# Turning the feed-forward's gated activations with VectorE blocks and a trip through DRAM, in place of TensorE transposes

## The chip, the cores and the metric

The kernel runs on one core of a Trainium2 chip, in one launch. The metric is the device time of that launch in microseconds (us), as the median of several runs. Beside it stands one profiled execution, whose span (first to last instruction) and own time are given; every view of the trace shown here comes from that execution.

## The reference

The reference is a trunk of two layers over 256 tokens of width 1024 in float32. A layer is a half-step feed-forward, a token mixer (gated DeltaNet beside a causal Conformer convolution), and a second half-step feed-forward, each between an RMS norm ahead and one behind. Cut to what the change concerns:

```python
def swiglu_ffn(h, w_in, w_out):
    gate, up = jnp.split(h @ w_in, 2, axis=-1)      # h: 256 x 1024, w_in: 1024 x 5632
    return (jax.nn.silu(gate) * up) @ w_out         # w_out: 2816 x 1024

for i in range(DEPTH):                              # DEPTH = 2
    f = swiglu_ffn(rmsnorm(x, ffn1_norm_pre[i]), ffn1_w_in[i], ffn1_w_out[i])
    x = x + 0.5 * rmsnorm(f, ffn1_norm_post[i])
    ...                                             # the token mixer
    f = swiglu_ffn(rmsnorm(x, ffn2_norm_pre[i]), ffn2_w_in[i], ffn2_w_out[i])
    x = x + 0.5 * rmsnorm(f, ffn2_norm_post[i])
```

There are thus four feed-forwards. The product `silu(gate) * up` comes out with tokens on the partitions, and the second matrix product needs it as the stationary operand, with its 2816 channels on the partitions: it has to be transposed.

## The kernel before

**Products.** Every float32 product is made of three TensorE products of rounded parts: a value is split into a high part (rounded to the fast 32-bit format, on ScalarE) and a low part (the rest, by a subtraction). `mm3` is high x high, high x low, low x high.

**Weights.** `Stream` brings all weights in pieces of 128 x 1024 floats (512 KB). The order of the pieces is fixed. A piece is loaded by SP into one of 4 buffers `raw`, cast by ScalarE into `whi` and subtracted by VectorE (in the mixer partly by GpSimd) into `wlo`; `whi` and `wlo` are rings of 8. When TensorE is done with a piece, `done()` writes down the load of the piece eight further on. SP's queue is thus a line of loads, each waiting for the buffer that was read four pieces earlier.

**A feed-forward.** `proj_in` goes over 11 chunks of 512 columns (256 of gate and 256 of up). A chunk takes 4 pieces; each piece is multiplied for both halves `tb` of the tokens, 12 matmuls of 512 columns in all, so a chunk is 48 matmuls. At a chunk's end `ev` reads the sums from PSUM: ScalarE takes the silu, VectorE multiplies by up, into a tile `ag` for each `tb`. `fin` then adds the steps of the lane "ffn", which transposes the two `ag` tiles in four 128 x 128 blocks on TensorE into a PSUM tile `tr`, and splits that into `act[c]` (high part on ScalarE, low part on VectorE). `proj_out` multiplies the 22 blocks of `act` (two per chunk) by 22 pieces of the second weight; it comes behind all 11 chunks, and takes `act[0]` first.

**Order.** TensorE's instructions stand in the order in which they are written; the other engines' queues are ordered by a scheduler, by priorities. `lanes.tick()` is called 16 times a chunk and runs the steps that are due; `DELAY["ffn"]` says after how many ticks: 34 before, so the transposes of a chunk stand a little over two chunks behind it. GpSimd (`W`) has nothing of a chunk to do in the feed-forwards.

**Names.** In the trace line 143 is `Products.matmul`, 149 is `Products.transpose`, 123 is `Clocked` (VectorE and GpSimd), 170 is `Held` (ScalarE), 269 the load of a piece. The tiles: `mm` PSUM sums, `xt` the transposed input, `raw`, `whi`, `wlo` the pieces, `w1i`, `w1o`, `w2i`, `w2o` the feed-forwards' weights in DRAM, `mw` those of the mixer. The mixer has some trips through DRAM of its own: `dA<-at`, `ia<-dA`, `dU<-iu`, `u<-dU`.

Of the kernel before, what the change touches and what calls it, by code (L numbers as in the profile page):

```python
# [9 lines left out]
F32 = mybir.dt.float32  # L10
# [3 lines left out]
ALU = mybir.AluOpType  # L14

P = 128
# [26 lines left out]
]  # L43

DELAY = {
    "first": (1, 2), "ffn": (34, 4, 3, 17, 8, 11, 48, 40), "pre0": (13, 7, 8, 4, 3, 3), "pre1": (15, 16, 0, 13, 8),
    "yt0": (10, 0, 10, 10, 26), "yt1": (10, 2, 0, 3, 3), "f_g0": (5, 0, 2, 1), "f_g1": (5, 1, 1, 1), "c0": (0, 0),
    "f_k1": (0, 1, 3, 1, 1, 3), "f_ka": (2, 0, 3), "decays": (12, 4, 2, 15, 4), "dts": (51, 3, 0, 0, 19, 19),
# [24 lines left out]

POOL = {5, 7, 8, 11, 13, 16, *range(18, 21), 23, *range(29, 33), 35, 36, *range(39, 45), *range(47, 50), 51, 53, 55, 58, 60, 61, 63, 65, 67, 68, *range(70, 73), 77, 78, 84, 85}

CFG = dict(stat=500, conv=50, ev=300, tok=4, st=4, post=-800, pre=1000, fin=None, tokens=-100, glu=100, dec=200, dts=-100, kt=-400, vt=1000, qt=50, inv=1000, sim=100, merge=-400, scan=50, norm=200, onorm=-100, yt=-400, w=50, tails=4, ahead=1.5, lag=6, free=3, aheadp=3, lag2=3, bias=2, held=1)

KIND = {"f_g0": "glu", "f_g1": "glu", "f_g2": "glu", "f_g3": "glu", "decays": "dec", "dts": "dts", "kt0": "kt", "kt1": "kt",
        "vt0": "vt", "vt1": "vt", "qt0": "qt", "qt1": "qt", "qs": "qt", "inv": "inv", "sim0": "sim", "sim1": "sim",
# [97 lines left out]
class Lanes:  # L177
# [33 lines left out]
    def tick(self):  # L211
# [5 lines left out]
        for job in list(self.jobs):  # L217
            if job in self.jobs and not any(job[1] in f for f in FILL) and job[0] <= self.now and self.ready(job):
                self.step(job)
        for eng, names, ahead in zip(self.engines, FILL, (CFG["ahead"], CFG["aheadp"])):  # L220
            while eng.at < self.pe.at + ahead:
# [20 lines left out]
def prio(tc, key):  # L242
    return nullcontext() if key is None or not CFG[key] else tc.high_priority(offset=CFG[key])


class Stream:
# [16 lines left out]
    def load_one(self, parts=1):  # L263
# [9 lines left out]
        def high(c):  # L273
            with prio(self.tc, "w"):
                self.act.copy(hi[:, c], raw[:, c])

        def low(c, eng):
            with prio(self.tc, "w"):
                eng.tensor_tensor(lo[:, c], raw[:, c], hi.bitcast(F32)[:, c], op=ALU.subtract)

        if self.lanes is not None:
            c = slice(0, n)
            self.his.append((self.lanes.now + CFG["lag"], i, lambda: high(c)))
            self.lows.append((self.lanes.now + CFG["lag"] + CFG["lag2"], i, lambda eng: low(c, eng)))
            return
# [7 lines left out]
    def tick(self, upto=-1):  # L293
# [5 lines left out]
        while self.lows and due(self.lows[0]):  # L299
            job = self.lows.pop(0)  # L300
            first = self.gp.at + 2.4 <= self.vec.at + 1.2 + CFG["bias"] and job[1] < len(self.side) and self.gp.tc is not None
            job[2](self.gp if first else self.vec)
# [21 lines left out]
def trunk(ctx: ExitStack, tc: tile.TileContext, x_in, wfirst, consts, feat, pch, tokp,  # L324
          w1i, w1o, mkb, mkc, mw, w2i, w2o, out, depth=NL):
    nc = tc.nc
# [7 lines left out]
    dram = ctx.enter_context(tc.tile_pool(name="dram", bufs=1, space=bass.MemoryType.DRAM))  # L334

    def slot(i, shape, dt=F32, name=None):
        return slots.tile(shape, dt, name=name or f"s{i}", tag=f"s{i}")
# [4 lines left out]
    def tokt(name="tok", shape=None, dt=F32):  # L342
        return work.tile(shape or [P, 512], dt, name=name, tag="tok", bufs=CFG["tok"])

# [6 lines left out]
    def ps_tr(shape=None):  # L351
        return psum.tile(shape or [P, 4, P], F32, name="tr", tag="tr", bufs=3)
# [6 lines left out]
    T = Products(nc.tensor)  # L359
    V, S, W = Clocked(nc.vector, vector_us), Held(nc.scalar, T), Clocked(nc.gpsimd, pool_us)  # L360
# [5 lines left out]
    def load_feat(l, r, si):  # L366
        t = slot(si, [P, D], name="wbc")
        nc.sync.dma_start(t, feat[l, r:r + 1, :].broadcast_to([P, D]))
        return t
# [22 lines left out]
    ident = cst[:, K_ID:K_ID + P]  # L392
# [27 lines left out]
    def split(hi, lo, src):  # L420

        S.copy(hi, src)
        V.tensor_tensor(lo, src, hi.bitcast(F32), op=ALU.subtract)
# [105 lines left out]
    def post(tb, acc, wbc, half, fws, jks):  # L529
        fw = slot(fws, [P, D], name="fw")  # L530
        jk = slot(jks, [P, D], name="jk")
        ss = small(2, "ss2")
        for hf in range(2):
            cs = slice(hf * 512, hf * 512 + 512)
            S.activation(jk[:, cs], acc[hf], AF.Square, scale=D ** -0.5, accum_out=ss[:, hf:hf + 1])
            V.scalar_tensor_tensor(fw[:, cs], acc[hf], half, wbc[:, cs], op0=ALU.mult, op1=ALU.mult)
        r = small(1, "rpost")
        rms_scale(r, ss[:, 0:1], ss[:, 1:2])
        for hf in range(2):
            cs = slice(hf * 512, hf * 512 + 512)  # L540
            V.scalar_tensor_tensor(x[tb][:, cs], fw[:, cs], r, x[tb][:, cs], op0=ALU.mult, op1=ALU.add)
# [68 lines left out]
    def proj_out(lhs, nkt, ev, tails=None, need=None):  # L610
        tails = CFG["tails"] if tails is None else tails
        acc = [[ps_mm(), ps_mm()] for _ in range(2)]

        def go(kt, tb, w, halves=(0, 1)):
            ah, al = lhs(kt, tb)
            for hf in halves:
                cs = slice(hf * 512, hf * 512 + 512)
                mm3(acc[tb][hf], ah, al, w[0][:, cs], w[1][:, cs], kt == 0, kt == nkt - 1)
                lanes.tick()
        tail = nkt - RING  # L620
        kt = 0
        while kt < tail:
            b = min(2, tail - kt)
            for tb in range(2):
                for j in range(b):
                    go(kt + j, tb, st.peek(j))
            for j in range(b):
                st.done()
            kt += b
        for hf in range(2):  # L630
            for j in range(RING):
                go(tail + j, 0, st.peek(j), (hf,))
        with prio(tc, "post"):
            ev(0, acc[0])
        if need:
            lanes.finish(need())
        for j in range(RING - tails):
            go(tail + j, 1, st.peek(0))
            st.done()
        for hf in range(2):  # L640
            for j in range(tails):
                go(nkt - tails + j, 1, st.peek(0 if hf else j), (hf,))
                if hf:
                    st.done()
        with prio(tc, "post"):
            ev(1, acc[1])


    def ffn(xt, l, wpost, after, first=2, tails=None):
        act = []  # L650
        gated = {}

        def ev(c, tb, ps):
            a = tokt("ag", [P, 2, 256])
            S.activation(a[:, 0, :], ps[:, 0:256], AF.Silu, scale=xt[tb][1])
            V.scalar_tensor_tensor(a[:, 1, :], ps[:, 256:512], xt[tb][1], a[:, 0, :], op0=ALU.mult, op1=ALU.mult)
            gated[c, tb] = a

        def fin(c):
            act.append(slot(c, [P, 2, 2, 2, P], F32R, name="act"))  # L660

            def steps():
                tr = ps_tr([P, 2, 2, P])
                for tb in range(2):
                    a = gated.pop((c, tb))
                    for k in range(2):
                        T.transpose(tr[:, k, tb, :], a[:, 1, k * P:(k + 1) * P], ident)
                with prio(tc, "fin"):
                    split(act[c][:, 0], act[c][:, 1], tr)
                yield  # L670
            lanes.add("ffn", steps())

        proj_in(xt, [(512, 2)] * 11, ev, fin, first)
        wbc = load_feat(l, wpost, 17)

        def lhs(kt, tb):
            t = act[kt // 2]
            return t[:, 0, kt % 2, tb, :], t[:, 1, kt % 2, tb, :]

        def done(tb, acc):  # L680
            post(tb, acc, wbc, 0.5, 11 + tb, 13 + tb)
            after(tb)

        proj_out(lhs, 22, done, tails)
# [680 lines left out]
    st = Stream(tc, nc, ring, pieces, side, S, V, W)  # L1365
    xt = start()
    for l in range(depth):
        ffn(list(xt), l, R_F1POST, make_pre(l, R_MPRE, 18, 15, norm=True), first=2 if l else 0)
        mixer(list(xt), l, make_pre(l, R_F2PRE, 0, 6))

        def last(tb):
            for hf in range(2):
                cs = slice(hf * 512, hf * 512 + 512)
                nc.sync.dma_start(out[tb * P:(tb + 1) * P, cs], x[tb][:, cs])
        ffn(list(xt), l, R_F2POST, make_pre(l + 1, R_F1PRE, 18, 15) if l + 1 < depth else last,
            tails=None if l + 1 < depth else 4)
# [73 lines left out]
```

## Time and profile before

| | |
|---|---|
| median of 3 runs | 1379.19 us (1376.68 to 1379.22) |
| the profiled execution | 1378.3 us, of which its span is 1376.5 us |
| granted TensorE clock, mean | 0.997 |
| busy: TensorE, its weight loads | 1352.0 us (98%), 1148.0 us (83%) |
| busy: VectorE, ScalarE, GpSimd | 907.9 us (66%), 735.7 us (53%), 367.7 us (27%) |
| moved by DMA | 250.67 MB, mean 182 GB/s; the kernel's queues on SP take 56.0% of the 16 DMA engines |

Matmuls are pipelined, so a busy TensorE says little by itself: its pace is read from the distance between the starts of its instructions. "Idle before" is the time in which an engine stood still ahead of an instruction, with the instruction that released it. Idle time of an engine that nobody waits for costs nothing. SPq is SP's queue, from which DMAs are issued.

### The profile page before, as it was taken

Reading aid. Unit: us, or ns where it says so; the run is one execution under the profiler, and the core shown is the slowest. Engines: PE = TensorE matmul, PEld = TensorE weight load, DVE = VectorE, ACT = ScalarE, POOL = GpSimd, SP = SyncE. Lnnn points to the kernel's source line nnn. Section 1 sums busy time; section 2 is a strip of 40 time slices with the busy share of each in tenths; the row PEclk is TensorE's granted clock in tenths of the full one; section 3 lists DMA queues with packets and bytes.
Section 4 is the critical chain, followed back from the end, with each engine's and each line's share of the span. In section 5 each row is a group of like instructions: output and inputs, shape, how many; then the busy total and the mean of one; then the engine's idle time right before and its main releaser. Section 6 shows DMA issues by size and latency. Waiting matters only on the chain.

```text
span 1376.5 us, 20079 instructions
## 1 busy us (share of the span) xinstructions
PE 1352.0 (98%) x7435; PEld 1148.0 (83%) x7435; DVE 907.9 (66%) x1549; ACT 735.7 (53%) x1172; POOL 367.7 (27%) x328
## 2 busy tenths in 40 slices
PE   9999999998999999999999999999989999999998
PEld 6888879997887878888888888799978878888886
DVE  6655456999966676555475554569999666755543
ACT  6544447666555455444364443567656564654441
POOL 0000015798743200000000000267996432000000
PEclk9999999999999999999999999999999999999999
DMA  8866555553634657555476566365546446565551
GB/s 288 259 185 184 179 160 201 184 187 113 200 123 138 232 202 227 185 184 176 146 253 195 186 181 189 129 230 168 178 133 187 145 136 227 170 230 186 188 178 42
DMA packets 82962, 250.67 MB, mean 182 GB/s; under 512 B 21136, under 2 KB 21680, under 8 KB 82864
## 3 DMA queue, kind: packets, MB, share of 16 engines
q1 hardware_dynamic: 82576, 249.32, 56.0%
q8 instruction: 58, 0.95, 0.3%
q14 instruction: 40, 0.33, 0.1%
q10 hardware_dynamic: 288, 0.07, 0.0%
HBM read 245.14 MB, written 4.21 MB: 181 GB/s over the span
## 4 chain that ended last, share of the span: by engine, by line
PE 90%; DVE 6%; ACT 1%; DMA 1%; issue 1%; POOL 0%; DVEq 0%; POOLq 0%; ACTq 0%
PE mm L143 82%; PE gd L143 4%; PE tr L149 4%; DVE wlo L123 2%; DVE c L123 2%; DVE cacc L123 1%; DMA raw<-mw 1%; ACT whi L170 1%; PE gd L149 0%; ACT cf L170 0%; ACT vr L170 0%; DVE x L123 0%; DVE xt L123 0%; DVE fw L123 0%; ACT vT L170 0%
## 5 line engine op out<-in xcount | busy, mean ns | idle before, releaser
L170 ACT CAST whi<-raw 128x1024 fp32r<-128x1024 f32 (+2 forms) x445 | 461.9, 1043 | 404.9 <-PE mm L143 318.8
L143 PE MATMUL mm<-whi,xt 128*128 128x512 f32 (+1 forms) x2048 | 657.4, 393 | 5.4 <-ACT qT L170 2.2
L123 DVE TENSOR_TENSOR wlo<-raw,whi 128x1024 fp32r<-128x1024 f32 (+1 forms) x341 | 415.0, 1223 | 293.5 <-ACT whi L170 287.3
L143 PEld LDWEIGHTS mm<-whi,xt 128*128 128x128 f32 x2048 | 382.7, 188 | 86.1 <-DVE xt L123 5.7
L143 PE MATMUL mm<-wlo,xt 128*128 128x512 f32 (+1 forms) x1024 | 396.7, 387 | 0.7 <-DVE wlo L123 0.7
L123 POOL TENSOR_TENSOR wlo<-raw,whi 128x1024 fp32r<-128x1024 f32 (+1 forms) x104 | 247.2, 2394 | 142.7 <-ACT whi L170 140.4
L143 PEld LDWEIGHTS mm<-wlo,xt 128*128 128x128 f32 x1024 | 193.0, 188 | 36.8 <-DVE wlo L123 1.4
L143 PE MATMUL mm<-whi,act 128*128 128x512 f32 x704 | 221.8, 392 | 0.0
L123 POOL TENSOR_TENSOR rpost<-ss,exp 128x1 f32<-128x1 f32 x12 | 6.5, 540 | 701.1 <-DVE ss L123 701.1
L123 DVE SCALAR_TENSOR_TENSOR cacc<-hT,pc,cacc 128x254 f32<-128x254 f32 (+28 forms) x464 | 179.3, 463 | 0.2
L143 PE MATMUL mm<-xt,whi 128*128 128x256 f32 x960 | 175.1, 284 | 0.6 <-DVE c L123 0.3
L143 PEld LDWEIGHTS mm<-whi,act 128*128 128x128 f32 x704 | 132.2, 188 | 27.4
L143 PEld LDWEIGHTS mm<-xt,whi 128*128 128x128 f32 x960 | 149.4, 192 | 1.4 <-ACT qT L170 0.9
L143 PE MATMUL mm<-wlo,act 128*128 128x512 f32 x352 | 137.0, 389 | 0.0
L143 PE MATMUL mm<-xt,wlo 128*128 128x256 f32 x480 | 135.8, 283 | 0.0
L143 PEld LDWEIGHTS mm<-xt,wlo 128*128 128x128 f32 x480 | 92.0, 192 | 0.0
L143 PEld LDWEIGHTS mm<-wlo,act 128*128 128x128 f32 x352 | 66.2, 188 | 13.3
L170 ACT ACTIVATE ag<-mm,rstd 128x256 f32<-128x256 f32 x88 | 37.7, 472 | 22.7 <-PE tr L149 18.6
L170 ACT ACTIVATE jk<-mm 128x512 f32<-128x512 f32 x24 | 14.4, 598 | 62.3 <-PE mm L143 62.3
L123 DVE SCALAR_TENSOR_TENSOR fw<-mm,wbc 128x512 f32<-128x512 f32 x24 | 16.5, 687 | 46.4 <-ACT jk L170 46.4
L123 DVE SCALAR_TENSOR_TENSOR c<-mm,pc,c 128x255 f32<-128x255 f32 (+2 forms) x108 | 43.7, 474 | 3.4 <-ACT c L170 3.4
L143 PE MATMUL mm<-whi,yt 128*128 128x512 f32 x128 | 41.4, 394 | 0.0
(188 smaller groups left out, 1171.7 us busy)
## 6 DMA issues: line engine op xcount, KB each, us to landing
raw<-mw SPq DMA_DIRECT2D x168, 512.0 KB, 3.8
raw<-w1i SPq DMA_DIRECT2D x88, 512.0 KB, 3.9
raw<-w2i SPq DMA_DIRECT2D x88, 512.0 KB, 4.1
raw<-w1o SPq DMA_DIRECT2D x44, 512.0 KB, 3.6
raw<-w2o SPq DMA_DIRECT2D x44, 512.0 KB, 3.3
wbc<-feat SPq DMA_DIRECT2D x13, 512.0 KB, 4.8
raw<-mkb SPq DMA_DIRECT2D x8, 272.0 KB, 3.0
xs<-x SPq DMA_DIRECT2D x4, 512.0 KB, 2.6
```

Source lines behind the costliest of these rows:

```text
L123: r = op(out, *a, **k)
L143: r = self.eng.matmul(o, w, x, **k)
L149: r = self.eng.transpose(*a)
L170: r = op(*a, **k)
```

## The change

The lane "ffn" no longer uses TensorE. For each chunk VectorE transposes the two `ag` tiles in 32 x 32 blocks into the first half of a tile `way`. Inside a group of 32 partitions the blocks are then turned, but each block still lies in the wrong group of partitions. Four DMAs (one for each group of 32 partitions, 64 KB each, in rows of 512 bytes) write the groups to a DRAM tile `turned`, and one DMA (256 KB, 2 KB for each partition) reads it back into the second half of `way`, with every block in its place. ScalarE casts the high part from `way`, and GpSimd, no longer VectorE, subtracts the low part. All five DMAs go through SP's queue, among the loads of the pieces. The delays become 3 ticks to the first step, 5 to the read, 12 to the split. (`prio` with "turn" or "fin" has no effect, both are None.)

```diff
-    "first": (1, 2), "ffn": (34, 4, 3, 17, 8, 11, 48, 40), "pre0": (13, 7, 8, 4, 3, 3), "pre1": (15, 16, 0, 13, 8),
+    "first": (1, 2), "ffn": (3, 5, 12), "pre0": (13, 7, 8, 4, 3, 3), "pre1": (15, 16, 0, 13, 8),
...
         def fin(c):
             act.append(slot(c, [P, 2, 2, 2, P], F32R, name="act"))

             def steps():
-                tr = ps_tr([P, 2, 2, P])
+                way = slot(11 + c % 4, [P, 2, 512], name="way")
+                out4 = way[:, 0].rearrange("p (j k b t) -> p k b j t", j=4, k=2, b=2)
                 for tb in range(2):
                     a = gated.pop((c, tb))
-                    for k in range(2):
-                        T.transpose(tr[:, k, tb, :], a[:, 1, k * P:(k + 1) * P], ident)
+                    with prio(tc, "turn"):
+                        V.transpose(out4[:, :, tb], a[:, 1, :].rearrange("p (k j c) -> p k j c", k=2, j=4))
+                turned = dram.tile([4, 32, 4, P], F32, name=f"way{l}{c}")
+                for i in range(4):
+                    nc.sync.dma_start(turned[:, :, i].rearrange("j c w -> c j w"),
+                                      way[32 * i:32 * i + 32, 0].rearrange("c (j w) -> c j w", j=4))
+                yield
+                nc.sync.dma_start(way[:, 1], turned.rearrange("j c i w -> (j c) (i w)"))
+                yield
+                src = way[:, 1].rearrange("p (i b t) -> p b i t", i=4, b=4)
+                hi, lo = (act[c][:, n].rearrange("p k b (i t) -> p (k b) i t", i=4) for n in range(2))
                 with prio(tc, "fin"):
-                    split(act[c][:, 0], act[c][:, 1], tr)
-                yield
+                    S.copy(hi, src)
+                    W.tensor_tensor(lo, src, hi.bitcast(F32), op=ALU.subtract)
             lanes.add("ffn", steps())
```

In the trace of the changed kernel line numbers from 659 on are higher by up to 12; the four writes are line 673, the read line 676.

**SP's queue, first feed-forward, about chunks 4 and 5, before.** Only loads of pieces stand there (`raw_748` is a buffer's number in the program).

```order
L269 DMA raw_748<-w1i 128x1024
L269 DMA raw_766<-w1i 128x1024
L269 DMA raw_784<-w1i 128x1024
L269 DMA raw_802<-w1i 128x1024
L269 DMA raw_836<-w1i 128x1024
```

The same stretch after; `way04` and `way05` are the DRAM tiles of chunks 4 and 5, `way_678` and `way_770` their tiles on the chip. The load `raw_691` is that of piece 28.

```order
L269 DMA raw_691<-w1i 128x1024
L673 DMA way04_681<-way_678 32x4x128 x4
L269 DMA raw_710<-w1i 128x1024
L269 DMA raw_728<-w1i 128x1024
L676 DMA way_678<-way04_681 128x512
L269 DMA raw_746<-w1i 128x1024
L269 DMA raw_783<-w1i 128x1024
L269 DMA raw_802<-w1i 128x1024
L673 DMA way05_773<-way_770 32x4x128 x4
L269 DMA raw_820<-w1i 128x1024
```

Four writes stand two loads ahead of the read of the same chunk, and two to four loads stand between a read and the next chunk's writes. The writes of chunk 4 stand ahead of the loads of pieces 29 and 30.

**VectorE's queue, about chunk 5, before**: the products of both halves follow each other, then the low part of the chunk two earlier, then the low parts of four pieces.

```order
L123 SCALAR_TENSOR_TENSOR ag_632<-mm_551,rstd0_99,ag_632 128x256
L123 SCALAR_TENSOR_TENSOR ag_635<-mm_552,rstd1_100,ag_635 128x256
L123 TENSOR_TENSOR act_462<-tr_647,act_462 128x512
L123 TENSOR_TENSOR wlo_662<-raw_660,whi_661 128x1024
L123 TENSOR_TENSOR wlo_680<-raw_678,whi_679 128x1024
```

After (chunk 5; `wlo_712` and `wlo_730` are pieces 29 and 30):

```order
L123 TENSOR_TENSOR wlo_693<-raw_691,whi_692 128x1024
L123 SCALAR_TENSOR_TENSOR ag_752<-mm_667,rstd0_99,ag_752 128x256
L123 STREAM_TRANSPOSE way_770<-ag_752 128x2x4x32
L123 TENSOR_TENSOR wlo_712<-raw_710,whi_711 128x1024
L123 SCALAR_TENSOR_TENSOR ag_755<-mm_668,rstd1_100,ag_755 128x256
L123 TENSOR_TENSOR wlo_730<-raw_728,whi_729 128x1024
L123 STREAM_TRANSPOSE way_770<-ag_755 128x2x4x32
```

The subtraction of `act` is gone from this queue, two block transposes have come in, and the second of them stands behind the low parts of the two pieces whose loads SP issues behind the writes of chunk 4. Outside the feed-forwards the order on all engines is the same before and after.

More of the change, by code (lines that the diff above doesn't have):

```diff
@@ L74 @@
 POOL = {5, 7, 8, 11, 13, 16, *range(18, 21), 23, *range(29, 33), 35, 36, *range(39, 45), *range(47, 50), 51, 53, 55, 58, 60, 61, 63, 65, 67, 68, *range(70, 73), 77, 78, 84, 85}
-CFG = dict(stat=500, conv=50, ev=300, tok=4, st=4, post=-800, pre=1000, fin=None, tokens=-100, glu=100, dec=200, dts=-100, kt=-400, vt=1000, qt=50, inv=1000, sim=100, merge=-400, scan=50, norm=200, onorm=-100, yt=-400, w=50, tails=4, ahead=1.5, lag=6, free=3, aheadp=3, lag2=3, bias=2, held=1)
+CFG = dict(stat=500, conv=50, ev=300, tok=4, st=4, post=-800, pre=1000, fin=None, turn=None, tokens=-100, glu=100, dec=200, dts=-100, kt=-400, vt=1000, qt=50, inv=1000, sim=100, merge=-400, scan=50, norm=200, onorm=-100, yt=-400, w=50, tails=4, ahead=1.5, lag=6, free=3, aheadp=3, lag2=3, bias=2, held=1)
 KIND = {"f_g0": "glu", "f_g1": "glu", "f_g2": "glu", "f_g3": "glu", "decays": "dec", "dts": "dts", "kt0": "kt", "kt1": "kt",
```

## The prediction

> **What bounds the kernel now.** I read the page first, then the chain of waits inside a feed-forward, then TensorE's timeline there, and last the waits of SP's queue. From the page, the busy times and the engines' shares of the chain that ended last; below them the chain from 90 to 114 us (start, length, what):
>
> ```profile
> PE 1352.0 (98%) x7435; PEld 1148.0 (83%) x7435; DVE 907.9 (66%) x1549; ACT 735.7 (53%) x1172; POOL 367.7 (27%) x328
> PE 90%; DVE 6%; ACT 1%; DMA 1%; issue 1%; POOL 0%; DVEq 0%; POOLq 0%; ACTq 0%
> ...
> 91.06 10.94 PE mm L143 x48
> 102.01 0.44 PE tr L149 x4
> 102.44 10.94 PE mm L143 x48
> 113.39 0.44 PE tr L149 x4
> ```
>
> In a feed-forward the chain is TensorE alone, without a gap: 48 matmuls of a chunk, four transposes of an earlier chunk, 48 matmuls. A chunk takes 113.39 - 102.01 = 11.38 us. What are the transposes worth in it? TensorE's timeline (start, length, instructions):
>
> ```profile
> 101.61 0.40 PE L143 MATMUL mm<-whi,xt 128*128 128x512 f32 x1
> 101.84 0.60 PE L149 MATMUL tr<-cst,ag 128*128 128x128 f32 x4
> 102.20 0.48 PE L143 MATMUL mm<-whi,xt 128*128 128x512 f32 x1
> 102.51 0.40 PE L143 MATMUL mm<-wlo,xt 128*128 128x512 f32 x1
> ...
> 105.51 0.62 PE L143 MATMUL mm<-whi,xt 128*128 128x512 f32 x2
> ...
> 112.31 0.62 PE L143 MATMUL mm<-whi,xt 128*128 128x512 f32 x2
> ```
>
> From 105.51 to 112.31 stand 30 matmuls and no transpose: 6.80 / 30 = 0.2267 us each, so 48 need 10.88 us. The four transposes therefore cost 11.38 - 10.88 = 0.50 us a chunk: 0.44 in the chain, and 0.06 by which the matmuls right behind them are slow (0.31 instead of 0.23 us from 102.20 to 102.51).
>
> ScalarE and VectorE keep pace by waiting for TensorE:
>
> ```profile
> 102.26 0.84 ACT L170 ACTIVATE ag<-mm,rstd 128x256 f32<-128x256 f32 x2 [0.53 <-PE tr L149]
> 106.61 1.05 ACT L170 CAST whi<-raw 128x1024 fp32r<-128x1024 f32 x1 [1.69 <-PE mm L143]
> 109.33 1.05 ACT L170 CAST whi<-raw 128x1024 fp32r<-128x1024 f32 x1 [1.67 <-PE mm L143]
> 102.91 0.87 DVE L123 SCALAR_TENSOR_TENSOR ag<-mm,rstd,ag 128x256 f32<-128x256 f32 x2
> 107.70 1.22 DVE L123 TENSOR_TENSOR wlo<-raw,whi 128x1024 fp32r<-128x1024 f32 x1 [1.52 <-ACT whi L170]
> SPq L269 <- DVE wlo L123: 732.5, 320, 13.0
> ```
>
> Each cast stands still for 1.67 us until TensorE has left the ring's slot; casts follow each other at 2.72 us, a piece. SP, ahead of a load, waits for the low part of the piece four earlier (732.5 us over 320 loads): its queue runs as far ahead as the buffers allow.
>
> **The change, part by part.** Durations of what goes and of the nearest relatives of what comes, by group (count | busy, mean ns | idle before):
>
> ```profile
> L149 PE MATMUL tr<-cst,ag 128*128 128x128 f32 x176 | 26.4, 273 | 0.0
> L123 DVE SCALAR_TENSOR_TENSOR ag<-mm,rstd,ag 128x256 f32<-128x256 f32 x88 | 38.9, 476 | 0.5 <-ACT ag L170 0.5
> L123 DVE TENSOR_TENSOR act<-tr,act 128x512 fp32r<-128x512 f32 x44 | 30.0, 681 | 0.9
> L170 ACT CAST act<-tr 128x512 fp32r<-128x512 f32 x44 | 25.8, 587 | 6.0 <-PE tr L149 6.0
> L170 ACT CAST whi<-raw 128x1024 fp32r<-128x1024 f32 x435 | 455.4, 1052 | 400.4 <-PE mm L143 315.9 <-DMA raw<-mw 44.4 <-DMA raw<-w1i 13.1
> L123 POOL TENSOR_TENSOR wlo<-raw,whi x104: 1363/2402/3417, 196.8 to 1155.3; 128x1024 fp32r<-128x1024 f32 x100, 128x544 fp32r<-128x544 f32 x4
> L123 DVE TENSOR_TENSOR wlo<-raw,whi x341: 677/1225/1981, 7.5 to 1349.2; 128x1024 fp32r<-128x1024 f32 x168, 128x544 fp32r<-128x544 f32 x2, 128x512 fp32r<-128x512 f32 x1
> 80.00:130.00 50.00, 50.00 (x229) 41.32 (x228) 27.96 (x33) 24.64 (x32) 0.00 (x0) 1.00 0.61 183
> ```
>
> *TensorE* loses 176 transposes, four in each of 44 chunks: 44 x 0.50 = 22.0 us, all on the path. The ends are 44 x 0.44 = 19.4 us (should the slow matmuls stay) and the busy sum, 26.4 us, which counts overlaps twice. I take 22.0, the measured distance between chunks.
>
> *VectorE* loses 44 subtractions (681 ns) and gets 88 block transposes, of which no row exists. The nearest row is the product of the same 128 x 256 elements, 0.48 us; ends 0.2 and 1.23 us (a low part, four times the elements). A chunk then takes 4 x 1.23 + 2 x 0.48 + 2 x 0.48 = 6.8 of 10.88 us. Cost nothing, under the matmuls; without that cover 88 x 0.48 - 30.0 = 12 us.
>
> *ScalarE* casts 512 elements from the chip's memory in runs of 32 instead of from PSUM: between 0.53 (half of the 1052 ns) and 1.05 us against 0.59; its chunk stays below 6.3 us. *GpSimd* gets 44 subtractions of about 1.2 us (half of 2402 ns); it had nothing in this stage (0.00 in the window's POOL column), and nobody needs `act` before `proj_out`. For the last chunk: its first use lies 14 pieces of 2.72 us and more behind the chunk's end, 38 us; its trip takes some 15 (4.0 + 1.8 + 2.7 + 0.4 + 3.5 + 1.1 + 1.2, all from rows here and below). Cost nothing.
>
> GpSimd's and VectorE's subtractions do disturb each other: the longest low parts are 1981 ns on VectorE and 3417 on GpSimd, 0.8 and 1.0 us over their medians. By such a row a chunk loses at most 1.2 us on VectorE, under 4 us that it has free.
>
> *SP and the DMAs* are the open part. Per chunk 4 writes and a read come into the line of loads. Their relatives in the mixer: the issues of `dA<-at` (ns min/median/max) and their landing; `u<-dU` (KB each, median us to landing); then loads of pieces from 60 to 120 us and from 1.5 to 12 us; the first 15 us (the last columns are clock, busy share of the DMA engines, GB/s); and SP's queue from 297 to 304 us, in the mixer's trips through DRAM (packets, MB, share):
>
> ```profile
> L928 SPq DMA_DIRECT2D dA<-at x16: 308/448/453, 296.9 to 982.1; - x16
> DMA to landing us min/median/max: 1.6/2.7/3.5
> u<-dU SPq DMA_DIRECT2D x16, 32.0 KB, 4.8
> raw<-w1i SPq DMA_DIRECT2D x16, 512.0 KB, 3.5
> raw<-w1i SPq DMA_DIRECT2D x5, 512.0 KB, 6.7
> 0.00:15.00 15.00, 11.62 (x42) 7.58 (x43) 6.97 (x23) 8.86 (x23) 0.20 (x4) 0.89 0.82 299
> q1 hardware_dynamic: 2380, 0.97, 61.4%
> ```
>
> `dA<-at`, 32 partitions to DRAM in rows of 128 bytes, is the nearest: 0.45 us to issue, 2.7 to land. A load lands 3.5 us after its issue in the steady stage, 6.7 in the crowd at the start. Let E be a chunk's end (102.01). The products are done at 102.91 + 0.87, E + 1.8; with two transposes and perhaps a low part between them the writes can go at E + 4.0 at the latest. The load of the second piece of the chunk three further on stands behind them. Before, it went when a low part was done, 2.3 us after TensorE left the second piece of this chunk, so at E - 5.4 + 2.3 = E - 3.1. Now it goes at E + 4.0 + 4 x 0.45 = E + 5.8, and lands at E + 9.3 + 0.3. Its cast was released at E + 5.4 (two pieces into the next chunk): 4.2 us late. A cast had been done, with its low part, 7 x 2.72 - 2.3 = 16.7 us ahead of need (seven pieces lie between release and use). So 12.5 us of spare stay, and TensorE does not wait. If that cover were gone, each us of lateness would be a us of the path.
>
> Can the lateness grow from chunk to chunk? The loop is: four writes, two loads, the second one's cast and low part, VectorE's second product and transpose behind it, the next chunk's writes. It takes 1.8 + 0.66 + 3.5 + 1.4 (512 KB behind another, at 299 / 0.82 = 365 GB/s) + 1.05 + 1.23 + 0.48 + 0.48 = 10.6 us, against a chunk of 10.88. Its ends: 9.2 without the 1.4, and 13.9 with a landing of 6.7 and 1.23 for product and transpose each. I take 10.6, since the steady stage is the nearest; it is close to the bound, and this is where I expect an error, if any. Volume: 4 x 512 KB at 183 / 0.61 = 300 GB/s (the window's last columns) are 7.0 us of the DMA engines, 512 KB more at the rate of the mixer's small rows (0.97 MB in 61.4% of the 7 us from 297 to 304, 226 GB/s) 2.3 us: 9.3 of 10.88.
>
> **Sum.** 1376.5 - 22.0 = 1354.5 us of span, with the 1.8 us around it 1356.3. The median of the runs lies 0.9 above the profiled execution; I say 1357.
>
> **Rivals.** (1) *The loop is longer than a chunk, and part of the gain is lost in waits for `wlo`.* With L for its length, lateness grows by L - 10.88 over nine turns; it exceeds 12.5 us from L = 12.3. At 12.6 each feed-forward waits 1.72 x 9 - 12.5 = 3.0 us, four of them 12: 1369. Above 12.9 the wait is more than a feed-forward's gain of 5.5 us, and the kernel slower: at the end of 13.9, (3.0 x 9 - 12.5) x 4 - 22 = 36 us. For it: the 6.7 us row. Against: the steady 3.5.
>
> (2) *Slower: the trip through DRAM itself holds SP's queue.* The read waits for the writes' landing R, and the loads behind it wait along. SP's line per chunk is 1.8 + R + 0.4 + 4 x 0.33 = 3.5 + R. A feed-forward is slower than before once (3.5 + R - 10.88) x 9 - 12.5 exceeds its gain of 5.5 us: R above 9.4 us. At R = 12 the four lose 116 us and win 22: 1472. Against: 2.7, at most 3.5 for rows four times shorter, 4.8 the slowest small transfer. For: none of these rows was written at this rate beside loads. The Trainium skill (VectorE: DVE Perf Modes, "The three transpose paths") warns that a plain DMA which transposes by strides is 19 times slower than the chip's transposing DMA when the innermost stride at the destination is large, and advises TensorE for 128 x 128. Here rows of 512 bytes stay whole. By that rule R would be 19 x 2.7 = 51 us, and the time above 2800; by the row it is 2.7, and the sum stays. No trace here shows such a slow transfer.
>
> (3) *Nothing is gained, the transposes lay in idle time*: 1378. Against: the 0.0 idle before them, and the chain.
>
> **Chances.** Forecast 0.74, its own range from 1376.7 - 22.0 = 1354.7 to 1379.2 - 19.4 = 1359.8; rival 1 0.13; rival 2 0.07; rival 3 0.03; 0.03 for what I don't see. A change of 0.2% (2.8 us) is about what a measurement of this kernel can tell. Faster: 0.74, most of rival 1 and of the rest, 0.86; same: rival 3 and a part of rival 1, 0.05; slower: 0.09. The range reaches from 1353.5 into rival 1, to 1367; above it lies 0.15.
>
> **What would show it.** In the profile after: chunks 10.88 us apart in the chain, no `tr<-cst,ag`, block transposes near 0.5 us, writes landing in about 3 us, SP waiting for VectorE ahead of each chunk's first write, no TensorE wait for `wlo` in the feed-forwards, and the mixer as long as before. Waits of `mm` for `wlo` or `whi` from the middle of a feed-forward on would mean rival 1; SP waiting for the landing of `way` over 9 us rival 2.

## The result

| | before | after |
|---|---|---|
| median of the runs | 1378.03 us (1376.68 to 1379.22, 4 runs) | 1356.83 us (1355.62 to 1357.81, 4 runs) |
| the profiled execution, and its span | 1378.3 us, 1376.5 us | 1356.38 us, 1354.4 us |
| mean granted clock | 0.997 | 0.998 |

The ratio is 0.9846 (95% interval 0.9829 to 0.9863): faster, by 18.9 to 23.6 us. The spans differ by 22.1 us.

The page of the kernel after: busy times, the engines' shares of the chain that ended last, and from the list of DMA issues (KB each, median us from issue to landing) the rows of `w1i` and of the new trip:

```profile
PE 1331.3 (98%) x7259; PEld 1132.3 (84%) x7259; DVE 926.9 (68%) x1593; ACT 730.8 (54%) x1172; POOL 446.4 (33%) x372
PE 81%; DVE 9%; POOL 3%; ACT 3%; issue 2%; DMA 1%; DVEq 0%; POOLq 0%; ACTq 0%
raw<-w1i SPq DMA_DIRECT2D x88, 512.0 KB, 4.7
way<-way SPq DMA_DIRECT2D x176, 64.0 KB, 1.8
way<-way SPq DMA_DIRECT2D x44, 256.0 KB, 4.8
```

TensorE has 176 instructions fewer and is still 98% busy: a shorter line of the same density. VectorE is 19 us busier, GpSimd 79. TensorE's share of the chain fell from 90% to 81%, but that is in the mixer, whose chain the profile follows through other engines; inside a feed-forward it is one piece (start, length, what):

```profile
77.78 50.32 PE mm L143 x222
```

50.32 / 222 = 0.2267 us a matmul, so 48 of them, a chunk, take 10.88 us, with nothing between chunks. Where along the program was the time won? The first and last start of one row of the mixer, before and then after:

```profile
L143 PEld LDWEIGHTS gd<-state,kT x32: 188/192/192, 402.4 to 1084.8; 128*128 128x128 f32 x32
```

```profile
L143 PEld LDWEIGHTS gd<-state,kT x32: 187/192/192, 397.3 to 1068.3; 128*128 128x128 f32 x32
```

The row stands behind the first feed-forward (402.4 - 397.3 = 5.1 us earlier) and again behind the third (16.5 us); the span ends 22.1 us earlier. That is 5.1 to 5.7 us for each feed-forward. The mixers give little: from the last product with `act` to the next feed-forward's first silu the two take 311.5 and 312.8 us, against 312.8 and 312.7 before.

What the new steps take: the tile `way` (ns min/median/max, first and last start), with the landing of its DMAs in us:

```profile
L673 SPq DMA_DIRECT2D way<-way x176: 303/428/2049, 28.2 to 1290.8; - x176
L123 DVE STREAM_TRANSPOSE way<-ag x88: 401/445/448, 26.2 to 1288.9; 128x256 f32<-128x256 f32 x88
L676 SPq DMA_DIRECT2D way<-way x44: 326/327/329, 31.5 to 1292.6; - x44
L170 ACT CAST act<-way x44: 609/617/624, 37.2 to 1298.3; 128x512 fp32r<-128x512 f32 x44
L123 POOL TENSOR_TENSOR act<-way,act x44: 1287/1818/2047, 37.9 to 1299.0; 128x512 fp32r<-128x512 f32 x44
DMA to landing us min/median/max: 1.6/1.8/6.0
```

SP's queue (us in total, times, longest), and the window of the steady stage (last columns: clock, busy share of the DMA engines, GB/s):

```profile
SPq L269 <- DVE wlo L123: 429.0, 205, 13.0
SPq L673 <- DVE way L123: 128.9, 44, 5.2
SPq L676 <- DMA way<-way: 18.1, 44, 2.4
80.00:130.00 50.00, 50.00 (x223) 41.40 (x222) 31.60 (x37) 25.01 (x32) 8.64 (x5) 1.00 0.78 256
```

SP used to wait 732.5 us for low parts ahead of loads. Now it waits 429.0 there and 128.9 ahead of the writes of a turned chunk: a part of what was spare in the line of loads has been spent on the turn. (Between a read and the next chunk's writes SP's timeline shows one to three loads, not two to four.) The read waits for the writes' landing 0.4 us a time (18.1 / 44). The DMA engines are 78% busy, against 61%.

That the loads come later is seen on ScalarE (in brackets the idle time before, and what ended it):

```profile
96.25 1.05 ACT L170 CAST whi<-raw 128x1024 fp32r<-128x1024 f32 x1 [3.85 <-DMA raw<-w1i]
104.56 1.05 ACT L170 CAST whi<-raw 128x1024 fp32r<-128x1024 f32 x1 [1.66 <-PE mm L143]
```

At 96.25 a cast waits 3.85 us for its load, where before every cast there waited for TensorE. Within the same chunk ScalarE has caught up and waits for TensorE again: the lateness comes and goes with each chunk, and TensorE does not see it.

### The profile page after: what moved, and what is told of

Its sections match the earlier page's. It is cut to its first block, busy times and chain, and to the rows that moved or that the text cites. A ratio compares the mean times of both kernels' runs of the same rounds, so it can differ in the third digit from the quotient of the medians.

```text
span 1354.4 us, 20203 instructions
## 1 busy us (share of the span) xinstructions
PE 1331.3 (98%) x7259; PEld 1132.3 (84%) x7259; DVE 926.9 (68%) x1593; ACT 730.8 (54%) x1172; POOL 446.4 (33%) x372
## 2 busy tenths in 40 slices
DMA packets 114644, 273.76 MB, mean 202 GB/s; under 512 B 24656, under 2 KB 47728, under 8 KB 114544
## 4 chain that ended last, share of the span: by engine, by line
PE 81%; DVE 9%; POOL 3%; ACT 3%; issue 2%; DMA 1%; DVEq 0%; POOLq 0%; ACTq 0%
PE mm L143 75%; PE gd L143 4%; DVE cacc L123 3%; DVE c L123 3%; PE tr L149 2%; POOL wlo L123 2%; DVE wlo L123 2%; DMA raw<-mw 1%; ACT whi L170 1%; POOL rk L123 1%; DVE at L123 1%; ACT dt L170 1%; PE gd L149 0%; ACT sg L170 0%; ACT cf L170 0%
## 5 line engine op out<-in xcount | busy, mean ns | idle before, releaser
L143 PE MATMUL mm<-whi,xt 128*128 128x512 f32 (+1 forms) x2048 | 648.4, 392 | 4.8 <-ACT qT L170 2.3
L123 DVE TENSOR_TENSOR wlo<-raw,whi 128x1024 fp32r<-128x1024 f32 (+1 forms) x341 | 425.0, 1258 | 199.3 <-ACT whi L170 193.5
L143 PE MATMUL mm<-whi,act 128*128 128x512 f32 x704 | 218.3, 390 | 0.0
L123 POOL TENSOR_TENSOR act<-way,act 128x512 fp32r<-128x512 f32 x44 | 78.6, 1785 | 406.1 <-ACT act L170 396.4
L170 ACT ACTIVATE ag<-mm,rstd 128x256 f32<-128x256 f32 x88 | 41.8, 475 | 91.3 <-PE mm L143 75.2
L123 DVE SCALAR_TENSOR_TENSOR ag<-mm,rstd,ag 128x256 f32<-128x256 f32 x88 | 42.4, 481 | 54.0 <-ACT ag L170 53.8
L123 DVE SCALAR_TENSOR_TENSOR fw<-mm,wbc 128x512 f32<-128x512 f32 x24 | 16.5, 687 | 46.4 <-ACT jk L170 46.4
```

Of the source, the lines that this page charges most:

```text
L123: r = op(out, *a, **k)
L143: r = self.eng.matmul(o, w, x, **k)
L170: r = op(*a, **k)
```

## The experiments

Edits are against the changed kernel, which was itself timed again beside the first of them: 1355.57 us, ratio 0.9843 (0.983 to 0.9857).

> The changed kernel again, as the measure for the three runs beside it. Theory (the four TensorE transposes of a chunk, 0.50 us in the path, are the whole change): ratio to before 0.984 to 0.985, span 1354 to 1355 us.

**The trip left out.**

```diff
-                for i in range(4):
-                    nc.sync.dma_start(turned[:, :, i]..., way[32 * i:32 * i + 32, 0]...)
                 yield
-                nc.sync.dma_start(way[:, 1], turned...)
                 yield
-                src = way[:, 1].rearrange(...)
+                src = way[:, 0].rearrange(...)
```

This leaves out the move across groups of partitions: the blocks stay in the groups in which VectorE left them.

> The changed kernel without the trip through DRAM: the five DMAs of a chunk are left out and the high and low parts are taken from the tile that holds the block transposes, so the blocks stay in the wrong groups of partitions. Theory (the trip lies wholly under TensorE's matmuls): the same time as the changed kernel, 1354 to 1355 us of span, within 0.1%. Rival (the trip still costs something in SP's queue, in late weights or in memory traffic): 3 us or more faster than the changed kernel, a span under 1351.5 us.

1354.63 us, ratio 0.9835 (0.9822 to 0.9849), against 0.9843 (0.983 to 0.9857) with the trip. The steady stage:

```profile
80.00:130.00 50.00, 50.00 (x222) 41.42 (x222) 29.77 (x35) 25.48 (x32) 6.77 (x5) 1.00 0.65 195
```

The DMA engines fall back from 0.78 to 0.65, the time stays. The medians differ by 0.9 us for all the DMAs of the program; the two intervals can't tell that from nothing, and would also allow 3 or 4 us.

**Transposes put back on TensorE.** Four per chunk, of the constant matrix, whose result nobody reads:

```diff
+                tr = ps_tr([P, 2, 2, P])
+                for tb in range(2):
+                    for k in range(2):
+                        T.transpose(tr[:, k, tb, :], ident, ident)
```

> The changed kernel with four 128 x 128 transposes of a constant added to TensorE for every chunk, at the place of the block transposes; nothing reads their result and they wait for no data. Theory: TensorE's queue is the path, and the transposes themselves also slow the matmuls right behind them, so all of the 22.0 us come back: span 1376.4 us, a chunk every 11.38 us. Rival A (the 0.06 us a chunk came from ScalarE and VectorE reading the transposed tile in PSUM): 44 x 0.44 = 19.4 us come back, span 1373.8. Rival B (the gain came from VectorE or ScalarE being relieved, not from TensorE): nothing comes back, 1354.

1378.8 us, ratio 1.0017 (1.0008 to 1.0025): the whole gain is gone. The chain of that run, 90 to 114 us:

```profile
93.14 0.44 PE tr L149 x4
93.58 10.94 PE mm L143 x48
104.52 0.44 PE tr L149 x4
```

104.52 - 93.14 = 11.38 us a chunk, exactly the distance before. Since these transposes wait for nobody and nobody for them, their place in TensorE's line is the price: 0.44 in the chain, and the 0.06 by which the 48 matmuls behind them take 10.94 us and not 10.88. Over the medians it is (1378.8 - 1355.6) / 44 = 0.53 us a chunk. Rival 3 of the prediction, transposes in idle time, falls.

**The low part of `act` on VectorE**, as before the change (`W.tensor_tensor` becomes `V.tensor_tensor`):

> The changed kernel with the low part of the activations subtracted on VectorE, as before, instead of on GpSimd. Theory (both engines have room in the feed-forwards): the same time as the changed kernel within 0.1%; VectorE's low parts of the weights lose their long tail over 1.9 us in the feed-forwards. Rival (GpSimd's subtractions are needed for the gain, VectorE being near its limit): 2 us or more slower than the changed kernel. Rival (the two engines' mutual waiting costs time): 2 us or more faster.

1356.06 us, ratio 0.985 (0.9837 to 0.9864): the same. The low parts of the weights from 20 to 130 us, of the changed kernel timed beside it and then of this one, and this one's subtraction of `act`:

```profile
L123 DVE TENSOR_TENSOR wlo<-raw,whi x46: 1185/1225/2177, 20.2 to 129.3; 128x1024 fp32r<-128x1024 f32 x46
```

```profile
L123 DVE TENSOR_TENSOR wlo<-raw,whi x46: 1183/1225/1227, 20.0 to 129.2; 128x1024 fp32r<-128x1024 f32 x46
L123 DVE TENSOR_TENSOR act<-way,act x44: 647/683/693, 37.2 to 1297.5; 128x512 fp32r<-128x512 f32 x44
```

The longest low part falls from 2177 to 1227 ns once GpSimd does not subtract beside it, and the subtraction takes 683 ns on VectorE, where GpSimd took 1818 (1287 at best). The two engines do hold each other up. It costs nothing, under the matmuls.

**SP's line held.** Two small trips through DRAM (16 KB each), each waiting for the one before, put into SP's queue per chunk:

```diff
+                for i in range(2):
+                    small_trip = dram.tile([P, 32], F32, name=f"held{l}{c}{i}")
+                    nc.sync.dma_start(small_trip, held)
+                    nc.sync.dma_start(held, small_trip)
```

> The changed kernel with two more round trips through DRAM for every chunk in SP's queue, small ones (16 KB to DRAM, read back into the same tile, each waiting for the one before), so that SP's line is held and hardly any traffic is added. By the loads and trips of the profile a small trip holds the line about 4.8 us (0.4 and 0.4 to issue, 1.8 and 2.2 to land). Theory (weights run about 12.5 us ahead of need, and lateness grows only by what a chunk's line exceeds 10.88 us): the line takes 1.8 + 2 x 4.8 = 11.4 us, lateness grows by 0.5 x 9 = 5 us, under the spare: no loss, 1354 to 1358 us. Rival (the weights have no such spare; any hold of the line is paid): 11 chunks x 4 x some us, over 1400 us.

1371.26 us, ratio 0.9942 (0.9919 to 0.9966): 15.7 us of the gain are gone, and the expectation of no loss was wrong. SP's queue: the writes of the third and of the eleventh chunk, in the changed kernel and then in this one (start, length); and of this one the wait of the reads, the trips' landing, and the first long wait of TensorE:

```profile
47.95 1.77 SPq L673 DMA_DIRECT2D way<-way  x4
135.19 1.77 SPq L673 DMA_DIRECT2D way<-way  x4
```

```profile
48.41 1.35 SPq L675 DMA_DIRECT2D way<-way  x3
146.60 1.40 SPq L675 DMA_DIRECT2D way<-way  x3
SPq L682 <- DMA held<-held: 142.9, 71, 6.6
DMA to landing us min/median/max: 1.4/2.7/8.2
120.95 0.50 PE L143 MATMUL mm<-wlo,xt 128*128 128x512 f32 x1 [0.77 <-DVE wlo L123]
```

The writes come every (135.19 - 47.95) / 8 = 10.9 us in the changed kernel, TensorE's pace, and every (146.60 - 48.41) / 8 = 12.27 us here: SP's line has become longer than a chunk, and its lateness grows by 1.4 us a chunk.

How much of that is hidden can be read from the lead of a low part: the time from its end to the start of the first matmul that reads it. (Low parts and matmuls take the pieces in the same order, so they can be paired.) The first piece of the eleventh chunk, in the changed kernel, and then VectorE's row here (TensorE's is the last one above):

```profile
102.93 1.23 DVE L123 TENSOR_TENSOR wlo<-raw,whi 128x1024 fp32r<-128x1024 f32 x1 [0.26 <-ACT whi L170]
120.91 0.39 PE L143 MATMUL mm<-wlo,xt 128*128 128x512 f32 x1
```

```profile
119.68 1.22 DVE L123 TENSOR_TENSOR wlo<-raw,whi 128x1024 fp32r<-128x1024 f32 x1
```

The low part is done 120.91 - 104.16 = 16.8 us ahead of its use in the changed kernel, and 0.05 us ahead here. The lowest lead of each chunk in the first feed-forward, in us:

| chunk | 5 | 6 | 7 | 8 | 9 | 10 | 11 |
|---|---|---|---|---|---|---|---|
| before | 14.1 | 14.6 | 17.3 | 17.3 | 17.3 | 17.3 | 17.3 |
| changed kernel | 9.6 | 11.0 | 11.7 | 12.3 | 13.6 | 14.2 | 15.0 |
| two small trips | 6.6 | 5.4 | 3.7 | 2.1 | 1.4 | 0.1 | 0.1 |

So the line ate a lead of some 14 us before TensorE waited: from 20 to 120 us TensorE waits for no low part, and the row at 120.95 is the first that does.

What was lost then is not spread evenly over the four feed-forwards. The row of the mixer that was shown above, in this run:

```profile
L143 PEld LDWEIGHTS gd<-state,kT x32: 187/192/192, 410.1 to 1083.4; 128*128 128x128 f32 x32
```

It starts 12.8 us later than in the changed kernel in the first layer and 15.1 us later in the second; the span ends 16.0 us later. The first feed-forward loses 7.2 us, most of it in `proj_out`, and the mixer behind it about 6. The trips lie that way too, for the scheduler did not leave them in their chunks: 24 of the 88 start in the first feed-forward, 39 in the mixer behind it, 9 in each of the next two feed-forwards, none in the fourth. Those three lose nothing. The expectation was wrong in the length of the line (12.27 us, not 11.4) and in where the trips stand. What exactly the mixer waited for was not taken apart.

> The same with four small round trips a chunk. Theory: the line takes 1.8 + 4 x 4.8 = 21 us a chunk, each feed-forward waits (21 - 10.88) x 9 - 12.5 = 79 us, four of them 314: about 1670 us, TensorE waiting for low parts from the second half of proj_in on; this is the way in which the trip through DRAM would have made the kernel slower. If trips overlap more than that (2.5 us each), the line takes 11.8 us and nothing is lost. Rival (SP's line does not matter, loads are issued early enough): 1355 us.

With four such trips: 1387.2 us, ratio 1.0075 (1.0048 to 1.0102), slower than the kernel before. It did not reach the expected time, since the scheduler spread the trips over the whole program (87 of the 176 start in the two mixers), so this run does not price R. It does show the sign turn, with a wait that was nearly absent after the change (0.5 us):

```profile
PE mm L143 <- DVE wlo L123: 12.3, 19, 0.8
```

**A transpose by DMA alone.** In one chunk of the eleven (c = 5) the block transposes go, and 16 DMAs per feed-forward write `ag` to DRAM transposed, element by element:

```diff
+                            nc.sync.dma_start(turned[:, :, i, w0:w0 + 32].rearrange("j c t -> t (j c)"),
+                                              a[32 * i:32 * i + 32, 1, k * P:(k + 1) * P])
```

> The changed kernel in which, for chunk 5 of each feed-forward alone, VectorE's block transposes are left out and the DMAs to DRAM do the whole transpose: 16 writes of 16 KB each, every element of 4 bytes by itself. The result is the same. By the rule of the Trainium skill (VectorE: DVE Perf Modes, The three transpose paths: 19 times slower) the writes of the chunk would land after 19 x 2.4 = 46 us. Theory (a transfer of small rows is paid by the row: in the mixer's trips 2207 rows of 128 bytes took at most 31 ns of one DMA engine each): 65536 rows x 31 / 16 engines = 127 us for the chunk; SP's line is held for it, each feed-forward waits 127 - 17 = 110 us, so about 1355 + 440 = 1795 us. By the rule's 46 us: 1355 + 4 x 29 = 1471. Rival (element-wise writes are as good as rows of 512 bytes, VectorE's turn is not needed): 1355.

2673.03 us, ratio 1.9402 (1.9261 to 1.9543), far past every number expected. TensorE's wait, the 64 issues (ns), the landing of their DMAs (us), and a window in which nothing else runs:

```profile
PE mm L143 <- ACT whi L170: 1318.1, 5, 332.4
L675 SPq DMA_DIRECT2D way<-ag x64: 325/20534/34955, 76.2 to 2517.6; - x64
DMA to landing us min/median/max: 34.0/62.4/80.6
130.00:200.00 70.00, 0.00 (x0) 0.00 (x0) 0.00 (x0) 0.00 (x0) 0.00 (x0) 0.50 1.28 1
```

A single chunk stops a feed-forward for (2673.0 - 1355.6) / 4 = 329 us: 65,536 elements of 4 bytes take some 340 us (329 and a lead of 10 to 15 us), 5 ns each over all engines, at 1 GB/s. The four writes of the change move the same bytes in rows of 512 bytes and are landed within 1.77 + 1.8 = 3.6 us of the first issue, a factor of about 95. The issues alone, 20.5 us each at the median, hold SP, for 307.85 us in the first feed-forward; whether they or the DMA engines behind them set the pace is not separated.

**More volume.** Extra loads of 512 KB per chunk that nobody reads:

```diff
+                for i in range(4):
+                    spare = slot(19, [P, D], name="spare")
+                    nc.sync.dma_start(spare, w1i[l, 4 * c + i])
```

> The changed kernel with four more loads of 512 KB a chunk into a tile that nothing reads, in SP's queue behind the chunk's read: traffic alone. In proj_in the changed kernel moves 257 GB/s at 0.78 of the DMA engines' time, so they carry about 329 GB/s. Theory: 4.72 MB a chunk need 14.3 us, each feed-forward waits (14.3 - 10.88) x 9 - 12.5 = 18 us, four of them 73: about 1430 us, with the DMA share near 1 in proj_in. Rival (DMA engines have room for more, the limit is elsewhere): 1355 us.

1584.66 us, ratio 1.1502 (1.1462 to 1.1542), more than expected, because the edit did two things at once: all four loads share one buffer, so each waits for the one before, in SP's queue.

```profile
SPq L679 <- DMA spare<-w1i: 468.8, 163, 6.7
```

So it was taken apart: one load (its buffer long free), and two into two buffers.

> One more load of 512 KB per chunk, read by nobody, whose buffer has long been free when the next one comes; the volume alone grows, from 3 MB to 3.6 MB moved per chunk. If the DMA engines still have room (0.78 busy in the steady stage, so about 0.90 with this load), the time stays at 1355.6, at most 1358. If the volume is the limit already, each chunk gets longer by up to 1.4 us less the spare: 4 x (11 x 1.4 - 8) = 30 us, 1385.

1354.71 us, ratio 0.983 (0.9816 to 0.9845): nothing lost, though little was left to lose. In the first feed-forward the lowest lead of the last chunk is 1.4 us, against 15.0. (A chunk moves 4 x 512 + 4 x 64 + 256 KB = 2.5 MB, so this load makes it 3.0; the 3 and 3.6 MB of the expectation were too high.)

> Two more loads of 512 KB per chunk into two buffers, so that neither waits for the other. Busy time of the DMA engines per chunk: 0.78 x 10.88 = 8.5 us, with 2 x 1.4 us 11.3 us, against 10.88: the volume passes the chunk by 0.4 us, which 8 us of spare hide over 11 chunks, so 1355 to 1358. If the loss with four loads (1584.7) came from the volume, half of that volume should lose in proportion: some 100 us, 1450. If it came from the line (each load waiting for the buffer of the one before), this loses nothing or little.

1370.9 us, ratio 0.9949 (0.9932 to 0.9965): 15 us lost. The window of 20 to 130 us of the changed kernel, with one load, and with two, then SP's wait and the landing of `way` with two:

```profile
20.00:130.00 110.00, 110.00 (x487) 91.09 (x487) 72.83 (x87) 60.83 (x76) 17.04 (x10) 1.00 0.81 266
```

```profile
20.00:130.00 110.00, 110.00 (x487) 91.06 (x487) 70.22 (x80) 53.70 (x71) 14.54 (x10) 1.00 0.85 280
```

```profile
20.00:130.00 110.00, 107.44 (x469) 87.41 (x468) 67.06 (x80) 52.85 (x68) 10.96 (x8) 1.00 0.92 309
SPq L676 <- DMA way<-way: 76.8, 61, 4.0
DMA to landing us min/median/max: 1.6/4.2/7.1
```

At 0.85 busy DMA engines TensorE has its 487 matmuls, at 0.92 only 469. There the writes land in 4.2 us, not 1.8, and the read behind them waits 76.8 us, not 18.1: full DMA engines act through the line, as a longer R, and the lead in the first feed-forward is down to 0.1 us from the seventh chunk on. The same window with the four loads that share a buffer:

```profile
20.00:130.00 110.00, 94.08 (x378) 72.08 (x377) 51.52 (x63) 43.16 (x53) 7.70 (x6) 0.97 0.82 273
```

The DMA engines were less busy there (0.82) and moved less (273 GB/s) than with two loads (0.92, 309), and yet far more was lost: most of it came from loads waiting for each other, not from the volume.

**The same exchange in the mixer.** The 32 TensorE transposes of the V tokens give way to 8 block transposes of 128 x 512 on VectorE, 16 writes and 4 reads:

```diff
-                    T.transpose(tr[:, hl, :], vT[:, hl, tb * P:(tb + 1) * P], ident)
+                V.transpose(blk..., vT[:, :, tb * P:(tb + 1) * P]...)
+                nc.sync.dma_start(turned[:, :, i]..., blk[32 * i:32 * i + 32]...)
+            nc.sync.dma_start(back..., turned...)
-                    S.activation(t[:, th, :], tr[:, hl, :], ...)
+                    S.activation(t[:, th, :]..., back[:, :, th, :], ...)
```

> The same exchange in the mixer: the 32 TensorE transposes of the V tokens (tile vr, 8 of 128 x 128 in each of 4 places) go, and 8 VectorE block transposes of 128 x 512 with a trip through DRAM come. The theory that a transpose on TensorE costs its place in the line of matmuls (0.50 us for four) says 32 / 4 x 0.50 = 4.0 us less where TensorE alone is the path: 1355.6 - 4.0 = 1351.6. The theory that this holds only where VectorE has room says: in the mixer VectorE is busy throughout and stands on the chain, 8 transposes of about 0.9 us are 7 us of its time, so the gain is lost in part or wholly: 1354 to 1359, same as the changed kernel or slower than it by up to 3 us.

1393.13 us, ratio 1.0107 (1.0092 to 1.0122): 37 us worse than the changed kernel, and neither theory had that. First layer: VectorE's last block transpose, SP's writes, ScalarE and TensorE:

```profile
335.38 1.30 DVE L123 STREAM_TRANSPOSE vblk<-vT 128x512 f32<-128x512 f32 x2
341.22 4.11 SPq L1034 DMA_DIRECT2D vway<-vblk  x8
350.50 2.44 ACT L170 ACTIVATE vr<-vback,irk 128x128 f32<-128x128 f32 x8 [18.18 <-DMA vback<-vway]
353.63 2.08 PE L143 MATMUL gd<-qT,kT 128*128 128x128 f32 x8 [22.23 <-ACT sq L170]
```

The transposes are quick (0.65 us each) and done at 336.7. The writes stand in SP's queue until 341.2, the read lands at 350.3, and ScalarE, which works off its queue in order, stands 18.18 us at the scaling of `vr`. Behind that stands `sq`, for which TensorE waits 22.23 us. Two layers make 44 us. Here the consumer stood right behind the turn in ScalarE's queue, and other work behind the consumer; in the feed-forwards nobody needs `act` before the last matrix product.

So the wait was taken away and the turn kept: the read goes straight into `vr`, the queries' steps no longer come behind it, and the scalings stand later in ScalarE's queue.

```diff
-            back = slot(18 + gp, [P, 4, 8, 32], name="vback")
-            nc.sync.dma_start(back..., turned...)
+            for i in range(4):
+                nc.sync.dma_start(t[:, :, 32 * i:32 * i + 32], turned[:, :, i]...)
-    "vt0": (20, 5, 12, 4)
+    "vt0": (20,), "vs0": (26, 12, 2)
```

> The V tokens' turn once more, with the same block transposes and the same volume, but nothing waits on its landing: the read goes straight into the tile `vr` (four DMAs in rows of 128 bytes), the queries' steps no longer come behind it, and ScalarE's 16 scalings per layer stand further on in its queue, in place, beside the inverse. If the 37 us of the run before came from ScalarE's queue standing 18 us per layer on the landing of `vback`, with TensorE waiting 22 us for `sq` behind it, they go, and at best the 4.0 us of the transposes are won: 1351.6 to 1360. If VectorE's eight transposes (0.68 us each) or the volume were the cause, the time stays near 1393.

1361.51 us, ratio 0.9889 (0.9872 to 0.9905): 32 of the 37 us are back, so the standing queue was the cause. (The edit also lowers the priority of all these steps, `vt` from 1000 to -400, by which the scalings move back; the block transposes of the first layer start where they did, at 331.1 and 335.7 us, against 331.5 and 335.4.) By the medians it is still some 6 us over the changed kernel, by the profiled executions 2.7. What is left (ScalarE, and TensorE's waits):

```profile
337.07 1.08 ACT L170 ACTIVATE sq<-tr 128x512 f32<-128x512 f32 x2 [4.04 <-DVE vblk L123]
PE gd L143 <- ACT sq L170: 11.1, 4, 3.3
```

`sq` lies in the buffer of `vT`, which the block transposes read, and they stand in VectorE's full queue. TensorE waits 11.1 us for it: more than the 4.0 us of transposes that it no longer has. That this share is VectorE's and the buffer's was read from these rows, and not tried by itself.

## Why the prediction was right

The forecast was 1357.0 us, the median is 1356.8. That they meet to 0.2 us is luck: the four runs reach from 1355.6 to 1357.8, the same kernel later took 1355.6, and the 0.9 us that the forecast put between the profiled execution and the median came out as 0.45. The saving is not luck, as its parts show.

- **TensorE's saving** (22.0 us, 44 x 0.50) came out as 22.1 us of span. Both of its parts are shown: chunks 10.88 us apart without transposes, 11.38 with transposes that do nothing. No row `tr<-cst,ag` is left. The end of 19.4 us, slow matmuls that stay slow, is refuted by the pure 0.2267 us.
- **VectorE** (0.48 us a block transpose): 0.445. Its busy time rose by 19 us, not 12: the exchange makes 88 x 0.445 - 30.0 = 9, and the low parts of the weights grew by 10 (425.0 us on the page, 415.0 before). **ScalarE** (0.53 to 1.05 us): 0.617, so reading runs of 32 elements costs under 0.1 us against half of a piece's cast (0.53).
- **GpSimd** was mis-sized: 1.2 us was half of a larger subtraction's median; it takes 1.82 beside VectorE. Its mechanism was right, and the bound of 1.2 us a chunk held: at the most 2177 - 1225 = 0.95 us on a low part. In the timeline below VectorE starts 0.82 us before a GpSimd subtraction ends and takes 1.90 instead of 1.22 us, 0.68 longer. The Trainium skill (SBUF — State Buffer, "SBUF: two separate sides") says that a VectorE instruction with two inputs from the chip's memory and a GpSimd one share a pair of ports as an exclusive lock; these rows and the 1227 ns without it agree, nearly to the full 0.82 us.

```profile
91.25 2.00 POOL L123 TENSOR_TENSOR act<-way,act 128x512 fp32r<-128x512 f32 x1 [9.84 <-ACT act L170]
92.43 1.90 DVE L123 TENSOR_TENSOR wlo<-raw,whi 128x1024 fp32r<-128x1024 f32 x1 [0.34 <-ACT whi L170]
```

- **The writes** (0.45 us to issue, 2.7 to land): 0.43 and a median of 1.8 over all trips' DMAs; the bigger rows were cheaper than the nearest relative. The read (3.5 us, as a load) took 4.8, and the loads of `w1i` rose from 3.9 to 4.7 us (medians over all of them). The two errors have opposite signs.
- **The spare and the loop** were about right. Before, a low part was ready 17.3 us ahead of its use from the seventh chunk on (said: 16.7). After, the lowest lead of a chunk from the fifth on is 9.6 to 15.0 us in the first feed-forward, and 10.5 to 16.3 in the others (said: 12.5). It does not shrink from chunk to chunk but rises, from 11.0 in the sixth to 15.0 in the eleventh, 0.8 us a chunk; so the loop takes about 10.1 us, an estimate from these leads, where 10.6 was said. The error that the prediction looked for here did not come. Rival 1 is a real mechanism all the same: with two small trips the loop was 12.27 us, where the formula has the spare just used up, (12.27 - 10.88) x 9 = 12.5, and the lead reached 0.1 us in the tenth chunk. The formula leaves out the start: in the second chunk the lead of the first feed-forward is still building (2.9 us before, 2.8 after).
- **Rival 2** (R): the trip's DMAs land in 1.8 us at the median, and the read waits 0.4 us for it, 2.4 at the most, against the 9.4 that would turn the sign. The warning of the Trainium skill (VectorE: DVE Perf Modes, "The three transpose paths") is about strided transposes; where this study made one, the factor against rows of 512 bytes was about 95, not 19 (whose basis is another DMA). For a last dimension that isn't contiguous the skill (DMA: Bandwidth & Descriptors, "Rules for kernel authors") says that each element becomes a descriptor of its own. The trace agrees: its DMA packets rise from 114,644 to 375,508, about one for each of the 4 x 65,536 elements. The prediction's 51 us for R would have been too low for such a write. What keeps the change out of this is that VectorE turns inside 32 x 32 blocks, and the DMA moves only whole rows.
- **The volume** (9.3 of 10.88 us): 0.78 x 10.88 = 8.5 us. One more load per chunk is free over eleven chunks, two are not.

## What to carry to other kernels

Where TensorE's line is gapless, every instruction in it costs its distance, also an idle one, and can be moved to a slower path for nothing if its consumer stands far behind and each in-order queue that the path crosses has slack; read that slack as microseconds per loop turn and as the lead that the data has on its use, chunk by chunk, and test it by holding the queue. The same exchange loses where the consumer is near: look at what stands behind the waiting instruction on its own engine (here 22 us of TensorE behind an 18 us wait of ScalarE). Turn inside blocks on an engine and let the DMA move whole rows; a DMA that transposes single elements was about 95 times slower.

## What the runs showed that was not expected

- DMAs of 4-byte elements: 5 ns an element over all engines, 20.5 us of SP's time for an issue of 4,096 elements, which is 5 ns an element too.
- A run can lose nothing and yet have used up its spare: with one more load per chunk the time was the same, and the lowest lead 1.4 us.
- While TensorE stood still for long, its granted clock read 0.50 (the window of 130 to 200 us above). The first matmul behind a wait of 0.77 us took 0.50 us (the row at 120.95) where the others take 0.39.
- A small transfer is not quicker: 16 KB took 1.4 us at best and 2.7 at the median to land, each waiting for the one before among loads, and the 64 KB writes of the change 1.8 at the median.
- An instruction form that is fast alone doesn't tell what it costs in another place: a 128 x 512 block transpose takes 0.65 us on VectorE, and put into the mixer's queues it cost 37 us at first, 3 to 6 when nothing waited for its landing.
